# A Hymba block on one core: DVE evacuations behind each attention step's minimum, spread norm products, one key product with turned operands, and the last 256 tokens computed token-major

## The chip, the cores and the metric

The kernel runs on one core of a Trainium2 chip. TensorE (PE) multiplies, with its own weight-load queue (PEld); VectorE (DVE), ScalarE (ACT) and GpSimd (POOL) work element by element; SyncE (SP) issues nearly all DMA transfers. The metric is the device time of one execution in microseconds, the median of several runs. Lower is better.

## What is computed

One layer of a hybrid trunk on x of shape (1, 2048, 1024) in float32. Cut to what matters here:

```python
h = rmsnorm(x, norm_mix_g)
proj = h @ w_in                        # 1024 -> 512 (u) + 3 * 512 (q, k, v)
y_ssm = s5_mixer(u_ssm, ...)           # 32 groups, complex diagonal states, scan over time
y_att = chunked_attention(q, k, v, attn_rel_bias)   # 8 heads of 64; own 64-frame chunk and 8 before
x = x + concat(rmsnorm(y_ssm), rmsnorm(y_att)) @ w_out
h = rmsnorm(x, norm_ffn_g)
x = x + (silu(h @ w_gate) * (h @ w_up)) @ w_down    # inner width 2816
out = rmsnorm(x, norm_final_g)         # x * rsqrt(mean(x * x) + 1e-6) * g
```

## The kernel before

**Number format and layout.** Activations are held feature-major: features on the 128 partitions, tokens along the row. A float32 operand is split into a high part and a low part (`hi`, `lo`, in a rounded type), and a product is three matmuls, hi·hi, hi·lo and lo·hi (`mm3`, L76). `split` (L153) makes the two parts: ACT casts, DVE subtracts.

**Stages.** A state-space prologue runs to about 125 us, attention from there to about 700 us, the output projection to about 935 us, gate and up products to about 1780 us, and the down products to 2203 us. A tail of 37 us follows.

**Attention.** There are 128 steps: 4 blocks of 512 tokens, 4 head pairs, 2 heads, 4 query tiles. A step makes the scores of a query tile (2 to 4 matmuls into the bank `sc`, which has one buffer). One DVE instruction (L881) then adds the bias `nba` or `nbb`, writes the result `s` and leaves each row's minimum `mn`, and ACT takes the exponential (L884) with that minimum as its bias. In the same step PE transposes an earlier step's `s` (L79), ACT and DVE split the transposed tile into `pth` and `ptl` (L899, L900), and PE multiplies these with v. The bank `sc` is free for the next scores once L881 has read it.

**Fillers.** Between the parts of a step PE works on "units", generators that are advanced to a quota at each step by tables of step numbers:

- `hT_unit` prepares the next block's normalised input for eight feature tiles q = 0 to 7. It loads x, multiplies it by the gain and by 1/rms (L756, called the norm product here), casts to `hi` on ACT (L757) and subtracts to `lo` on DVE (L758). q = 0 to 2 have two sets of buffers, q = 3 to 7 have one. So `hi` 3 to 7 of the next block can be written only after the current block's last product that reads them.
- `qk_unit` makes the queries and the keys of a head pair (24 matmuls each, in a bank `pf` of two), then evacuates them. In the first block a DVE product with 1/rms comes first (`yt`, L791). Then ACT copies the high part and DVE subtracts the low part (L800 and L801 for q, L806 and L807 for k). A query's halves are copied to the other 64 partitions by DMA.
- `v_unit` does the same for v (L838 to L842). In the first block weights arrive raw (`raw`, two buffers, L702), are split (L153) and are written back for later blocks (`wss`). The v weights of the second half of the heads are pieces 9 and 11.
- The state-space units run their scans on POOL and a few products on PE.

**What sets the order.** PE's order is the order of the program text (`keep_in_program_order`). DVE, ACT, POOL and SP are ordered by a scheduler, by readiness and priority. An engine runs its instructions strictly in that order, so one that waits holds up all behind it.

**The tail.** The down products of the second half's last four slices run by token ranges: `TAIL = (0, 512), (512, 256), (768, 256)`. In each range `down` makes eight feature tiles and DVE adds each to `acc` (L1582). ACT squares it (L1596, L1599) and DVE sums the squares (L1600). `sums` multiplies them by ones on PE, and `newton` (L98 to L111) takes the inverse root on DVE with 14 small instructions: a first guess by integer arithmetic and three rounds. PE spreads it over the partitions (`no`), ACT copies it, and eight DVE products (L1612) and eight DMAs (L1613) finish the range:

```python
def products(self):
    pb = next(self.r)
    rs = self.rs or pb
    for i, a in enumerate(self.acc):
        v = a[:, self.ts]
        nc.vector.scalar_tensor_tensor(v, v, k.go[:, i : i + 1], rs[:, : self.n], op0=ALU.mult, op1=ALU.mult)
        nc.sync.dma_start(io["out"][i * P : (i + 1) * P, self.out], a[:, self.ts])
```

For the last range these two steps come after the last down product, with nothing else left for PE.

## Time and profile before

| | us |
|---|---|
| three runs | 2241.45, 2242.87, 2247.27 |
| median | 2242.87 |
| profiled execution | 2241.38 |
| its span | 2239.6 |
| what lies around the span | 1.8 |
| mean granted PE clock | 0.988 |

PE is busy nearly everywhere: of 40 equal slices of the span only a few show less than nine tenths, and these lie before 700 us and at the end. Its mean granted clock is read as a share of full speed; a stretch of idle time is sometimes followed by a stretch at a lower clock. Idle time of DVE, ACT and POOL costs nothing by itself. Read for each place which engine's wait ends last.

### The profile page before, as it was taken

The numbers are of one execution on the slowest core, as the hardware profiler recorded it, in microseconds if no ns is written. First come the engines' busy times: TensorE is split into PE (matmuls) and PEld (weight loads), VectorE is DVE, ScalarE is ACT, GpSimd is POOL, SyncE is SP. The second block draws the span as 40 slices with busy tenths as digits, with TensorE's granted clock in tenths as the row PEclk, the third lists the DMA queues.
The fourth block names the chain that finished last, engine by engine and source line by source line (L and its number), as shares of the span: only waits on it lengthen the run. The fifth ranks groups of instructions, "written<-read, shape, count | busy, mean of one in ns | idle before, by whom it ended". The sixth has DMA issues, their size and how long they took to land.

```text
span 2239.6 us, 30165 instructions
## 1 busy us (share of the span) xinstructions
PE 2153.6 (96%) x10632; PEld 1819.1 (81%) x10632; DVE 1543.1 (69%) x2706; ACT 1004.6 (45%) x1667; POOL 354.1 (16%) x830
## 2 busy tenths in 40 slices
PE   8988898999988999999999999999999999999997
PEld 6777797999977788788888887888888788888886
DVE  8756767555557666767766768767665577688776
ACT  6355565556567541443333335333333343353322
POOL 3354666666600000000000000000000100000000
PEclk9999999999999999999999999999999999999999
DMA  9778867666552436835645557546333495465642
GB/s 330 231 249 283 270 207 229 193 196 193 179 175 99 137 116 206 275 118 173 198 153 200 198 191 258 199 160 207 108 115 97 136 371 198 159 226 183 217 174 76
DMA packets 194664, 430.16 MB, mean 192 GB/s; under 512 B 19792, under 2 KB 38272, under 8 KB 187408
## 3 DMA queue, kind: packets, MB, share of 16 engines
q1 hardware_dynamic: 186768, 403.26, 54.3%
q0 software_dynamic: 7744, 24.97, 3.6%
q8 instruction: 83, 1.36, 0.3%
q14 instruction: 69, 0.57, 0.1%
HBM read 288.95 MB, written 131.10 MB: 188 GB/s over the span
## 4 chain that ended last, share of the span: by engine, by line
PE 81%; DMA 7%; DVE 6%; ACT 2%; issue 2%; SPq 1%; DVEq 0%; ACTq 0%
PE X L76 20%; PE ps L76 18%; PE pf L76 11%; PE Y L76 10%; PE big L76 7%; PE W L76 5%; PE pj L76 4%; PE pt L79 2%; PE sc L76 2%; DMA acc<-x 1%; DMA hd<-wc 1%; DMA x<-xt 1%; DMA lo<-hc 1%; DMA w<-wss 1%; DVE ptl L900 0%
## 5 line engine op out<-in xcount | busy, mean ns | idle before, releaser
L76 PE MATMUL X<-hi,c 128*128 128x512 f32 x1408 | 450.9, 391 | 6.5 <-DVE c L153 3.4
L76 PE MATMUL ps<-hd,hd 128*128 128x512 f32 (+1 forms) x1968 | 428.1, 379 | 3.3 <-DVE hd L153 2.0
L76 PEld LDWEIGHTS ps<-hd,hd 128*128 128x128 f32 x1968 | 356.4, 188 | 73.6 <-DVE hd L153 2.7
L76 PEld LDWEIGHTS X<-hi,c 128*128 128x128 f32 x1408 | 264.9, 188 | 63.6 <-DVE c L153 4.5
L76 PE MATMUL X<-lo,c 128*128 128x512 f32 x704 | 274.7, 390 | 0.0
L153 ACT CAST hd<-hd 128x1536 fp32r<-128x1536 f32 (+1 forms) x106 | 147.5, 1394 | 231.0 <-DMA hd<-hq 174.6
L76 PE MATMUL Y<-hi,c 128*128 128x512 f32 x704 | 225.2, 390 | 2.4 <-DVE u L1428 2.4
L153 DVE TENSOR_TENSOR hd<-hd 128x1536 fp32r<-128x1536 f32 (+1 forms) x106 | 174.1, 1644 | 38.6 <-ACT hd L153 38.3
L1532 POOL DMA_DIRECT2D hd<-hq x7 | 5.3, 757 | 1165.3 <-PE X L76 1151.2
L153 DVE TENSOR_TENSOR c<-S,c 128x512 fp32r<-128x512 f32 x176 | 120.9, 688 | 99.3 <-ACT c L153 99.0
L1424 ACT COPY u<-X 128x512 f32<-128x512 f32 x132 | 77.5, 588 | 197.4 <-PE X L76 197.3
L153 ACT CAST c<-S 128x512 fp32r<-128x512 f32 x176 | 109.4, 622 | 120.8 <-PE Y L76 61.8
L76 PE MATMUL big<-m,woh 128*128 128x512 f32 x512 | 161.5, 397 | 0.0
L76 PEld LDWEIGHTS Y<-hi,c 128*128 128x128 f32 x704 | 132.6, 188 | 31.0 <-DVE u L1428 3.2
L1566 DVE TENSOR_TENSOR acc<-acc,ps 128x512 f32<-128x512 f32 x196 | 130.1, 682 | 37.9 <-PE ps L76 37.7
L76 PEld LDWEIGHTS X<-lo,c 128*128 128x128 f32 x704 | 132.7, 188 | 27.4
L153 ACT CAST c<-raw 128x512 fp32r<-128x512 f32 x132 | 82.2, 623 | 150.2 <-PE Y L76 73.0
L76 PE MATMUL pf<-hi,w 128*128 128x512 f32 x416 | 148.7, 409 | 0.0
L76 PE MATMUL Y<-lo,c 128*128 128x512 f32 x352 | 137.2, 390 | 0.0
L900 DVE TENSOR_TENSOR ptl<-pt,pth 128x640 fp32r<-128x640 f32 (+3 forms) x152 | 98.3, 647 | 54.6 <-ACT pth L899 53.1
L884 ACT ACTIVATE s<-s,mn 128x640 f32<-128x640 f32 (+4 forms) x128 | 97.9, 765 | 61.9 <-DVE mn L881 58.6
L899 ACT CAST pth<-pt 128x640 fp32r<-128x640 f32 (+3 forms) x152 | 83.7, 551 | 83.2 <-PE pt L79 78.8
(451 smaller groups left out, 4269.1 us busy)
## 6 DMA issues: line engine op xcount, KB each, us to landing
w<-wss SPq DMA_DIRECT2D x36, 1024.0 KB, 6.2
hq<-g SPq DMA_DIRECT2D x140, 256.0 KB, 2.1
hd<-hq SPq DMA_DIRECT2D x35, 768.0 KB, 4.4
hd<-wc SPq DMA_DIRECT2D x35, 768.0 KB, 5.8
raw<-in_w_gate SPq DMA_DIRECT2D x44, 512.0 KB, 3.7
raw<-in_w_up SPq DMA_DIRECT2D x44, 512.0 KB, 4.1
wc<-px SPq DMA_DIRECT2D x66, 256.0 KB, 3.1
wss<-w SPq DMA_DIRECT2D x12, 1024.0 KB, 6.1
```

Source lines behind the costliest of these rows:

```text
L76: return self.tc.keep_in_program_order(self.tc.nc.tensor.matmul(*a, **b))
L79: return self.tc.keep_in_program_order(self.tc.nc.tensor.transpose(*a, **b))
L153: return nc.scalar.copy(hi, raw), nc.vector.tensor_tensor(lo, raw, f32(hi), op=ALU.subtract)
L884: nc.scalar.activation(s[:, :nk], s[:, :nk], AF.Exp, bias=mn[:], scale=-1.0, accum_out=sums[sb, pr][:, hh, qp : qp + 1])
L899: nc.scalar.copy(pth[:, a:b, qp, :], pt[:, a:b, :])
L900: nc.vector.tensor_tensor(ptl[:, a:b, qp, :], pt[:, a:b, :], f32(pth[:, a:b, qp, :]), op=ALU.subtract)
L1424: nc.scalar.copy(u[:], ps[:])
L1532: (nc.gpsimd if aside else nc.sync).dma_start(f32(lo), src.rearrange("g p c -> p g c"))
L1566: V.tensor_tensor(a, a, ps[:], op=ALU.add)
```

## The change

Five things change.

1. **`behind`.** Each step's L881 instruction is remembered in `k.least`. DVE instructions traced inside `behind()` are placed, in issue order only, after the most recent one: the splits of the v weights 9 and 11, the evacuations of q, k and v, and for the third and fourth block the norm products and the subtractions to `lo`.
2. **First block.** The raw v weights 9 and 11 are loaded two steps earlier, and their splits come a step apart.
3. **Third and fourth block.** The norm products of q = 3 to 7 are taken out of the loop with the casts: they run alone, spread over steps −20 to −10 before the block, and casts and subtractions follow in one step, −9. q = 0 to 2 move to steps −26 to −20.
4. **Last key product of a block** (`pr == 3`, `c == 1`): operands are read in the order q = 3 to 7, then 0 to 2.
5. **Tail.** The last 256 tokens are computed token-major by `by_tokens`, 128 tokens at a time: two banks of 512 features, into which PE also adds `acc` by a float32 product with the identity. The sum of squares comes from ACT's accumulation, the root from ACT's square root refined by four DVE instructions, and the rows go out through an output of their own (`out_t`). The other two ranges of the second half use `root` (ACT's square root and five DVE instructions) in place of `newton`. The final gain is loaded as a row on all partitions (`g_row`) before the tail, and a one-column square root ahead of it brings ACT's table.

```diff
+def root(k, pool, ps, n, w):
+
+    V = k.nc.vector
+    v, f, y, o = (k.t(pool, t, [P, w], bufs=2) for t in ("nv", "nf", "ny", "no"))
+    k.nc.scalar.activation(o[:], ps, AF.Sqrt, scale=1.0 / n, bias=k.eps)
+    V.tensor_scalar(v[:], ps, -0.5 / n, -0.5 * EPS, op0=ALU.mult, op1=ALU.add)
+    return refine(V, v, f, y, o)
+
+
+def refine(V, v, f, y, o):
+
+    V.reciprocal(y[:], o[:])
+    V.tensor_tensor(f[:], y[:], y[:], op=ALU.mult)
+    V.tensor_tensor(f[:], f[:], v[:], op=ALU.mult)
+    V.scalar_tensor_tensor(o[:], f[:], 1.5, y[:], op0=ALU.add, op1=ALU.mult)
+    return o
...
+        def behind(on=True):
+            return tc.issue_after(k.least) if on and k.least else nullcontext()
...
-                    with tc.high_priority(offset=-WAY):
+                    if n == 11:
+                        yield
+                    with tc.high_priority(offset=-WAY), behind(ns == (9, 11)):
...
+            def scaled(q):
+                with behind(sb > 1):
+                    nc.vector.scalar_tensor_tensor(xts[q], xts[q], k.gm[:, q : q + 1], S["rsn"][:, ts], op0=ALU.mult, op1=ALU.mult)
+
+            ahead = q0 and sb > 1
+            if ahead:
+                for q in range(q0, q1):
+                    yield
+                    scaled(q)
...
+                if not ahead:
+                    scaled(q)
+                nc.scalar.copy(hi[q], xts[q])
+                with behind(ahead):
+                    nc.vector.tensor_tensor(lo[q], xts[q], f32(hi[q]), op=ALU.subtract)
...
-                    for q in range(KT):
+                    qs = [*range(DB, KT), *range(DB)] if c and pr == 3 else range(KT)
+                    for n, q in enumerate(qs):
...
-                    nc.vector.tensor_tensor(t[:], ps[:], S["rsn"][:, :SB], op=ALU.mult)
+                    with behind():
+                        nc.vector.tensor_tensor(t[:], ps[:], S["rsn"][:, :SB], op=ALU.mult)
...
+                a, b = HTA if sb == 1 else HTE
+                units.append(Unit(hT_unit(sb, 0, DB), 2 + DB, g0 + a, g0 + b, 2))
+                gen, n = hT_unit(sb, DB), KT - DB
+                if sb > 1:
+                    units.append(Unit(islice(gen, 1 + n), 1 + n, g0 + HTE[1], g0 + HTM, 2))
...
+                    pre, mid = (6, (3, 2)) if c == 4 else (4, (2,))
...
+        def by_tokens(t0, hs, ds, acc):
+
+            ts = slice(t0, t0 + P)
+            m = (t0 // P) % 2
+            ps = [bank(dx) for _ in range(2)]
...
+            for c in range(2):
+                for n, ((hh, hl), (dh, dl)) in enumerate(zip(hs, ds)):
+                    mm3(te, ps[c][:], hh[:, 0, ts], hl[:, 0, ts], dh[:, 0, c * 512 : c * 512 + 512], dl[:, 0, c * 512 : c * 512 + 512], n == 0, n == len(hs) - 1, skip_group_check=True)
+                    if n == 0:
+                        for i in range(4):
+                            te.matmul(ps[c][:, i * P : (i + 1) * P], acc[4 * c + i][:, ts], k.ident[:], start=False, stop=False, skip_group_check=True)
+                    if n % 2:
+                        yield
...
+                    nc.scalar.activation(j[:], ps[c][:], AF.Square, accum_out=sq[c][:])
...
+                nc.scalar.activation(o[:], sq[1][:], AF.Sqrt, scale=1.0 / D, bias=f[:])
+                V.tensor_scalar(v[:], sq[1][:], -0.5 / D, y[:], op0=ALU.mult, op1=ALU.add)
+                refine(V, v, f, y, o)
+                nc.scalar.activation(ta, ta, AF.Copy, scale=o[:])
+                V.scalar_tensor_tensor(b[:], ps[1][:], o[:], g[:, 512:], op0=ALU.mult, op1=ALU.mult)
...
-        last.sums(True)
-        last.products()
+        for n, _ in enumerate(chain.from_iterable(by_tokens(t0, hs, ds, acc) for t0 in TOKENS)):
+            if n == 2:
+                last.sums(root=root)
+            if n == 5:
+                last.products()
```

The change moves instructions on DVE. The first place is the first block around step 12, where the scores of a new head pair meet the end of a key product. `yt` and `k` are the key's evacuation, `w` the subtractions of the v weights' split, and `s`, `mn` the step's minimum. DVE before:

```order
L900 TENSOR_TENSOR ptl_2115<-pt_2210,pth_2114 128x2x128
L791 TENSOR_TENSOR yt_2224<-pf_2069,rsn_91 128x512
L807 TENSOR_TENSOR k_406_1959<-yt_2224,k_406_1959 64x512
L807 TENSOR_TENSOR k_409_1962<-yt_2224,k_409_1962 64x512
L153 TENSOR_TENSOR w_2175<-raw_2073,w_2175 128x512 x2
L153 TENSOR_TENSOR w_2180<-raw_2075,w_2180 128x512 x2
L881 ISA s_2206,mn_2207<-sc_2203,nbb_1549 128x128
L881 ISA mn_2207 128x1
L881 ISA s_2247,mn_2248<-sc_2244,nbb_1549 128x256
```

And DVE after, at the same place:

```order
L942 TENSOR_TENSOR ptl_2116<-pt_2211,pth_2115 128x128
L175 TENSOR_TENSOR w_2128<-raw_1975,w_2128 128x512
L942 TENSOR_TENSOR ptl_2116<-pt_2211,pth_2115 128x2x128
L175 TENSOR_TENSOR w_2128<-raw_1975,w_2128 128x512
L175 TENSOR_TENSOR w_2133<-raw_1977,w_2133 128x512 x2
L922 ISA s_2207,mn_2208<-sc_2204,nbb_1550 128x128
L922 ISA mn_2208 128x1
L830 TENSOR_TENSOR yt_2225<-pf_2074,rsn_92 128x512
L922 ISA s_2248,mn_2249<-sc_2245,nbb_1550 128x256
L922 ISA mn_2249 128x1
L847 TENSOR_TENSOR k_406_1960<-yt_2225,k_406_1960 64x512
```

The key's three evacuations, which stood ahead of the minimum, now stand behind it; the four subtractions of `w` still stand ahead of it.

The second place is the end of the second block, where the third block's `lo` tiles and the last pair's keys are made. Here the scores of the next step need both `k` tiles. DVE before:

```order
L758 TENSOR_TENSOR lo_995_4534<-raw_4438,hi_994_4533 128x512
L900 TENSOR_TENSOR ptl_4418<-pt_4469,pth_4417 128x5x128
L910 RECIPROCAL rs_4625<-sm_4011 128x8
L756 SCALAR_TENSOR_TENSOR xt_5999<-xt_5999,g_mix_87,rsn_91 128x512
L758 TENSOR_TENSOR lo_997_4539<-raw_4438,hi_996_4538 128x512
L758 TENSOR_TENSOR lo_1015_4596<-raw_4440,hi_1014_4595 128x512
L807 TENSOR_TENSOR k_920_4236<-pf_4357,k_920_4236 64x512
L758 TENSOR_TENSOR lo_1017_4601<-raw_4440,hi_1016_4600 128x512
L881 ISA s_4515,mn_4516<-sc_4510,nba_97 128x640
L881 ISA mn_4516 128x1
L807 TENSOR_TENSOR k_923_4239<-pf_4357,k_923_4239 64x512
```

And after:

```order
L942 TENSOR_TENSOR ptl_4430<-pt_4475,pth_4429 128x5x128
L795 TENSOR_TENSOR lo_984_4503<-raw_3792,hi_983_4502 128x512
L795 TENSOR_TENSOR lo_986_4507<-raw_3792,hi_985_4506 128x512
L847 TENSOR_TENSOR k_930_4264<-pf_4374,k_930_4264 64x512
L795 TENSOR_TENSOR lo_988_4511<-raw_3794,hi_987_4510 128x512
L795 TENSOR_TENSOR lo_990_4515<-raw_3794,hi_989_4514 128x512
L847 TENSOR_TENSOR k_933_4267<-pf_4374,k_933_4267 64x512
L922 ISA s_4541,mn_4542<-sc_4536,nba_98 128x640
L922 ISA mn_4542 128x1
```

The norm product `xt` is gone from this place (it stands many steps earlier) and one `lo` fewer stands between `ptl` and the first `k`, but two `lo` and the second `k` now stand ahead of the next minimum.

The third place is the end of PE's queue. `ps` is the bank, `hd` the operands, `sa` and `sb` the sums of squares, `no` the inverse root. PE before:

```order
L76 MATMUL ps_19989<-hd_19522,hd_19526 128x256 x3
L76 MATMUL ps_19990<-hd_19522,hd_19526 128x256 x3
L76 MATMUL ps_20023<-ones_85,sa_19898 128x1
L76 MATMUL ps_20023<-ones_85,sb_19901 128x1
L79 MATMUL ps_20046<-ident_80,no_20031 128x128 x2
```

And after:

```order
L79 MATMUL ps_19916<-hd_19504,hd_19500 128x512 x3
L79 MATMUL ps_19916<-ident_80,acc_3276_18347 128x128
L79 MATMUL ps_19916<-ident_80,acc_3277_18348 128x128
L79 MATMUL ps_19916<-ident_80,acc_3278_18349 128x128
L79 MATMUL ps_19916<-ident_80,acc_3279_18350 128x128
L79 MATMUL ps_19916<-hd_19512,hd_19508 128x512 x3
L79 MATMUL ps_19916<-hd_19520,hd_19516 128x512 x3
L79 MATMUL ps_19916<-hd_19528,hd_19524 128x512 x3
```

PE's queue now ends with a down product: the products with ones and the transposes of `no` for the last range are gone, and four products of `acc` with the identity stand in each bank.

More of the change, by code (lines that the diff above doesn't have):

```diff
@@ L43 @@
 HTP = 2
+HTE, HTM, HTL = (-26, -20), -10, (-9, -8)
 PRO = 0, 0, 2, 2, 2, 2, 0, 0, 0
@@ new lines, in qk_unit @@
+                with behind():
+                    for hh in range(2):
+                        q2h, q2l, k2 = ts[hh]
+                        a = slice(hh * 64, hh * 64 + 64)
+                        o = slice(64 - hh * 64, 128 - hh * 64)
+                        if c == 0:
+                            ways = (a, o) if both and hh == 0 else (a,)
+                            for w in ways:
+                                nc.scalar.activation(q2h[w, :], ps[a, :], AF.Copy, scale=-0.125)
+                                nc.vector.scalar_tensor_tensor(q2l[w, :], ps[a, :], -0.125, f32(q2h[a, :]), op0=ALU.mult, op1=ALU.subtract)
+                            if len(ways) == 1:
+                                nc.sync.dma_start(f32(q2h[o, :]), f32(q2h[a, :]))
+                                nc.sync.dma_start(f32(q2l[o, :]), f32(q2l[a, :]))
+                        else:
+                            nc.scalar.copy(k2[a, -SB:], ps[a, :])
+                            nc.vector.tensor_tensor(k2[o, -SB:], ps[a, :], f32(k2[a, -SB:]), op=ALU.subtract)
+                            if sb < NSB - 1:
+                                nc.sync.dma_start(S["k"][sb % 2, 2 * pr + hh], f32(k2[:, -SB:]))
```

120 lines of the change are left out of this document (64 added, 56 removed).

## The prediction

> **What bounds the kernel now.** I read the page's busy shares first, then its chain of waits by engine.
>
> ```profile
> span 2239.6 us, 30165 instructions
> PE 2153.6 (96%) x10632; PEld 1819.1 (81%) x10632; DVE 1543.1 (69%) x2706; ACT 1004.6 (45%) x1667; POOL 354.1 (16%) x830
> PE 81%; DMA 7%; DVE 6%; ACT 2%; issue 2%; SPq 1%; DVEq 0%; ACTq 0%
> ```
>
> PE is busy for 96% of the span and has 81% of the chain. So the change can win in two ways: it fills places where PE waits, or it shortens what follows PE's last matmul. Attention's places are found with a table of windows (columns: stretch, its length, busy time and count of PE, PEld, DVE, ACT, POOL, then PE's clock, DMA share, GB/s) and with PE's rows in the timeline; a bracket there gives the idle time before the row and who ended it.
>
> ```profile
> 177.70:183.40 5.70, 0.00 (x0) 0.01 (x1) 4.83 (x10) 3.50 (x7) 5.21 (x16) 0.88 1.01 372
> 183.40:189.00 5.60, 5.57 (x26) 5.60 (x27) 1.28 (x4) 1.64 (x6) 4.97 (x12) 0.51 1.01 383
> 275.70:282.00 6.30, 6.30 (x35) 5.58 (x36) 5.08 (x9) 3.74 (x9) 1.30 (x3) 1.00 0.56 171
> 370.00:374.00 4.00, 4.00 (x15) 3.50 (x16) 3.47 (x6) 2.00 (x4) 3.88 (x6) 0.60 0.61 212
> 400.00:650.00 250.00, 249.69 (x1592) 229.01 (x1591) 135.75 (x245) 137.79 (x274) 138.81 (x351) 1.00 0.60 182
> ...
> 183.43 0.55 PE L76 MATMUL sc<-k,q2h 128*128 128x256 f32 x1 [5.74 <-DVE mn L881]
> 275.67 0.77 PE L79 MATMUL pt<-ident,s 128*128 128x128 f32 x5 [3.11 <-DVE ptl L900]
> 369.93 0.63 PE L76 MATMUL sc<-k,q2h 128*128 128x320 f32 x1 [4.08 <-DVE k L807]
> 385.92 0.76 PE L79 MATMUL pt<-ident,s 128*128 128x128 f32 x5 [1.41 <-DVE ptl L900]
> ```
>
> From 400 to 650 us PE stands still for 0.3 us, so nothing is to be won there. Before that there are four stalls, all ended by DVE: 5.74 us (A), 3.11 (B), 4.08 (C) and 1.41 (D). After A the clock granted is 0.51, after C 0.60, and after B's 3.11 us it stays 1.00. So a stall costs more than its length from somewhere between 3.1 and 4.1 us on.
>
> [...]
>
> **Stall A, first block.** Behind what did the minimum wait?
>
> ```profile
> 177.72 0.69 DVE L791 TENSOR_TENSOR yt<-pf,rsn 128x512 f32<-128x512 f32 x1
> 179.10 1.40 DVE L807 TENSOR_TENSOR k<-yt,k 64x512 fp32r<-64x512 f32 x2 [0.68 <-ACT k L806]
> 180.53 2.54 DVE L153 TENSOR_TENSOR w<-raw,w 128x512 fp32r<-128x512 f32 x4
> 182.99 0.28 DVE L881 CUSTOM_DVE_ANT_0 s<-sc,nbb 128x128 f32<-128x128 f32 x1
> ...
> 163.67 0.64 SPq L729 DMA_DIRECT2D wss<-w  x1
> 174.21 1.07 SPq L702 DMA_DIRECT2D raw<-in_w_v  x2
> ...
> raw<-in_w_v SPq DMA_DIRECT2D x4, 512.0 KB, 6.4
> ...
> 175.32 4.51 DMA nbb<-nbs
> 185.05 3.84 PE pf L76 x18
> 190.63 2.15 PE pf L76 x18
> ```
>
> DVE spent 177.72 to 183.07 on the key's evacuation (0.69 + 0.68 idle + 1.40) and on four subtractions of the split (2.54); only then came the minimum. By the order of the changed kernel the evacuation stands behind the minimum. The four subtractions still stand ahead of it, but their data come earlier: the raw loads stand in SP's queue right behind the write of `wss` at 163.67, so they go out near 164.3 and not at 174.21, and at the median 6.4 us from issue to landing they are there at about 171. The subtractions then fall into the steps around 173 to 177. What is left is the bias `nbb`, which lands at 175.32 + 4.51 = 179.8, perhaps 1 us sooner without the raw issues ahead of it. The minimum then ends at 179.2 to 180.0 and not 183.2: 3.2 to 4.0 us. The rest of the stall, 1.7 to 2.5 us, is below B's length, which kept the clock, so 18 matmuls cost 2.15 and not 3.84: 1.7 more. Sum 4.9 to 5.7; I take **5.0**, since the DMA share is 1.01 there and transfers can be late. Bounds: 0 if the raws land as late as before, 7.4 (5.74 + 1.7) if all of it goes.
>
> **Stalls B, C, D, third and fourth block.**
>
> ```profile
> L756 DVE SCALAR_TENSOR_TENSOR raw<-raw,g_mix,rsn x12: 739/746/2143, 230.0 to 383.6; 128x512 f32<-128x512 f32 x12
> 271.14 2.14 DVE L756 SCALAR_TENSOR_TENSOR raw<-raw,g_mix,rsn 128x512 f32<-128x512 f32 x1
> 274.03 0.85 DVE L756 SCALAR_TENSOR_TENSOR raw<-raw,g_mix,rsn 128x512 f32<-128x512 f32 x1
> 365.17 1.08 DVE L756 SCALAR_TENSOR_TENSOR xt<-xt,g_mix,rsn 128x512 f32<-128x512 f32 x1
> 366.17 2.99 DVE L758 TENSOR_TENSOR lo<-raw,hi 128x512 fp32r<-128x512 f32 x2
> 369.19 0.68 DVE L807 TENSOR_TENSOR k<-pf,k 64x512 fp32r<-64x512 f32 x1
> ```
>
> B: two norm products of the third block (271.14 and 274.03) run directly ahead of the `ptl` at 274.80 for which PE waits. In the changed order they stand some 20 steps before their block, each behind a minimum, and none is left here. Of 3.11 us I take **2.8**; bounds 0 and 3.11.
>
> C: ahead of the first `k` stand a norm product (1.08) and two `lo` (2.99). Now the product is gone and two `lo` remain, which start where the product did: `k` ends near 368.0 and not 369.87, so the stall falls from 4.08 to about 2.2, and below B's length the clock stays: 0.40 of the 4.0 us window at 0.60, 1.6 us. Against it stands a new cost: `lo` twice and the second `k` now stand ahead of the next minimum, where one `lo` stood; two instructions of 0.7 us, of which I charge 1.0. Sum 1.9 + 1.6 − 1.0 = **2.5**; bounds 0 and 5.7 (4.08 + 1.6). That `lo` 3 to 7 can start sooner, because the turned key product lets go of `hi` 3 to 7 earlier, is in this.
>
> D: the products at the fourth block's `x` tiles go the same way: 1.41 and a smaller wait of 0.3 beside it, 1.7; I take **1.5**; bounds 0 and 1.7.
>
> New: the moved products and subtractions take DVE time elsewhere. It has 135.75 us of work in the 250 us from 400 on, so they find room, and I charge 0.8; bounds 0 and 3. What hides the evacuations' delay of one minimum is PE's own work: a unit's product runs 24 matmuls while the other `pf` bank is read. Attention in all: 5.0 + 2.8 + 2.5 + 1.5 − 0.8 = **11.0**.
>
> Unchanged, since the order around them is: a wait for `Bst` of 2.6 us and three of 14.1 us in all for `ptl` in the output projection.
>
> ```profile
> PE pj L76 <- DMA Bst<-bsts: 2.6, 1, 2.6
> PE pt L79 <- DVE ptl L900: 14.1, 3, 6.6
> ```
>
> **The tail.**
>
> ```profile
> 961.06 5.44 PE X L76 x24
> 279.03 1.24 PE L76 MATMUL pj<-rsn,Bst 128*128 128x256 f32 x5
> 2207.59 0.65 PE L79 MATMUL ps<-ident,no 128*128 128x128 f32 x4 [1.21 <-DVE no L110]
> 2222.03 0.43 PE L79 MATMUL ps<-ident,no 128*128 128x128 f32 x2 [1.40 <-DVE no L110]
> 2222.21 3.12 PE L76 MATMUL ps<-hd,hd 128*128 128x256 f32 x24
> 2208.24 9.44 PE ps L76 x80
> 2229.75 0.16 DVE L108 TENSOR_TENSOR nf<-ny 128x2 f32<-128x2 f32 x1
> 2232.32 3.22 DVE L1612 SCALAR_TENSOR_TENSOR acc<-acc,g_final,ps 128x256 f32<-128x256 f32 x8 [0.85 <-PE ps L79]
> 2187.34 0.64 ACT L1599 ACTIVATE sg<-acc 128x512 f32<-128x512 f32 x1 [0.65 <-DVE sa L1600]
> L884 ACT ACTIVATION_READ_ACCUMULATOR s<-s,mn x128: 183/188/196, 129.5 to 694.9; 128x1 f32 x128
> ```
>
> PE's time: the last range's 96 matmuls of 256 columns at 0.1235 (between 9.44 / 80 = 0.118 in the chain and 3.12 / 24 = 0.130 in the timeline) are gone, 11.9 us. In their place come 48 of 512 columns at 5.44 / 24 = 0.227, 10.9 us, and 16 float32 products of 128 columns. A float32 matmul shows as two passes in this trace (the `pj` row: 1.24 us for 5 passes of 256 columns, about 0.215 from start to start), so 32 passes. For one of 128 columns I take half, 0.115, 3.7 us; bounds 3.2 (0.10) and 6.9 (0.215, if the width does not matter). Net −11.9 + 10.9 + 3.7 = +2.7 us. The wait of 1.40 for the middle range's root falls, since `root` has 5 small DVE instructions where `newton` has 14 and PE now has a bank of work ahead of it: net cost **1.3**. The wait of 1.21 for the first range's root falls in the same way: **1.2** won.
>
> After the last matmul: before, it ends at 2222.21 + 3.12 = 2225.33 and the last DVE product at 2232.32 + 3.22 = 2235.54, 10.2 us. Now follow a square of 512 columns with its accumulator (0.64 + 0.19), a one-column root (about 0.2, by the accumulator's read), four small DVE instructions at 0.2 from start to start, and one product of 512 columns (0.75 by the norm product), with about 0.1 for handing over: 2.7. Won **7.5**; the closing DMAs are two of 256 KB in place of eight of 128 KB, with a landing as long. Tail: 1.2 − 1.3 + 7.5 = **7.4**; bounds 2.5 (float32 passes at 0.215 and a chain of 4.4 us) and 8.5. The load of `g_row` ahead of the first gate operands and one load of ACT's table in front of the tail I cost at nothing, hidden behind PE's products; without cover they cost 1.6 and 1.3.
>
> **The sum.** 11.0 + 7.4 = 18.4 us less than the profiled execution's 2241.38 (span 2239.6 and 1.8 around it): 2223.0. That execution lies 1.5 below the median of 2242.87, so against the runs it is about 2224.5; I say **2225**.
>
> **The rivals.** (1) *Only the tail gains.* Stalls A to C come back under another name: the four subtractions of `w` still stand ahead of the minimum in the order, and the raws must land in a stretch where the DMA share is 1.01; in C `lo` still stands ahead of `k`. Attention then gives 0 to 3, the time is 2242.9 − 7.4 − 1.5 = 2234 (2231 to 2237). Against it: the raws go out 10 us earlier. Chance 0.17.
>
> (2) *The tail gives 3 only*, with the float32 passes at 0.215 and a longer end: 2242.9 − 11 − 3 = 2229. Chance 0.10; it lies within the range.
>
> (3) *Spread norm products run long.* The group above has a median of 746 ns and a maximum of 2143: one took 1.4 us longer, and POOL is at work through most of attention (138.81 of 250 us in the table). There are 16 such products now, spread to places where PE has no slack. If each costs half of that, 16 × 0.7 = 11, attention gives nothing: 2235. Against it: a product behind a minimum has most of a step to finish. Chance 0.08.
>
> [...]
>
> (4) *Slower: evacuations pile up at the bank `pf`.* Each of the 32 q and k products is now evacuated behind a minimum (0.9 us with its read). If PE always stood at the next bank for that long, 32 × 0.9 = 29 would be lost against 18 won: about 2254. It decides from 18.4 / 32 = 0.58 us a product on. Against it: the order shows few evacuations that changed sides, and there are two banks with 24 matmuls (5.4 us) between. Chance 0.05.
>
> **How the numbers follow.** Forecast 0.60, rivals 0.17, 0.10, 0.08 and 0.05. 0.3% of the median is 6.7 us, about what a measurement of this kernel can tell from no change; faster means below 2236.1. The forecast and rival 2 lie below it, of rivals 1 and 3 about two thirds: 0.60 + 0.10 + 0.16 = 0.86, of which I take off 0.03 for a cost that no row shows. Faster 0.83, same 0.10, slower 0.07. The forecast's own range is 2216 to 2231, from bounds of A, C and the tail; to hold the time 8 times in 10 it reaches up to rivals 1 and 3: **2215 to 2237**.
>
> **What would show it.** In the changed profile: the wait of 5.74 for the minimum shrinks below 3 us and the clock behind it stays at 1.00 (A); no norm product next to a `ptl` that PE waits for at 272 and 385 (B, D); a wait for `k` near 370 of about 2 us without a slower clock (C); about 2.7 us from the last matmul to the last DVE product (tail), and the last 16 float32 products at 0.115 a pass. It would be wrong if a new wait on `sc`, `pf` or `pt` of several microseconds appears in the second to fourth block, or if the raws still land after 177.

## The result, and the profile after

| | before | changed |
|---|---|---|
| six runs, median (us) | 2243.26 | 2233.45 |
| six runs, lowest and highest | 2241.45 and 2247.41 | 2226.24 and 2236.52 |
| profiled execution | 2241.38 | 2226.24 |
| span | 2239.6 | 2224.1 |

The ratio of the changed kernel to the one before is 0.9938, with an interval of 0.9924 to 0.9951: faster by 0.6%, or some 14 us. The two medians in the table lie closer together, 9.8 us, so the size is less sure than the direction. The profiled execution is the fastest of its six, 7 us below their median, and its span is 15.5 us shorter than the span before. The kernel before scatters too, from 2240.84 to 2249.61 us in the 36 runs beside the experiments, and its profile is one of its fast executions as well. The distance between the changed kernel's profile and its median is the main thing that the experiments had to explain.

The page of the changed kernel, span, busy shares and chain by engine:

```profile
span 2224.1 us, 30080 instructions
PE 2155.5 (97%) x10606; PEld 1817.2 (82%) x10606; DVE 1533.2 (69%) x2671; ACT 1008.0 (45%) x1675; POOL 355.7 (16%) x830
PE 82%; DVE 7%; DMA 5%; issue 2%; ACT 2%; SPq 1%; ACTq 0%; DVEq 0%
```

PE is busy 1.9 us longer than before in a span that is 15.5 us shorter, so about 17 us of its idle time are gone. Where the four stalls were, PE's rows of the timeline now read:

```profile
180.20 0.36 PE L79 MATMUL sc<-k,q2h 128*128 128x256 f32 x1 [2.70 <-DVE mn L922]
226.40 1.96 PE L79 MATMUL pj<-U,Bst 128*128 128x256 f32 x8 [0.41 <-DMA Bst<-bsts]
234.14 0.50 PE L79 MATMUL pj<-pth,v 128*128 128x512 f32 x1 [2.14 <-ACT pth L941]
361.20 0.41 PE L79 MATMUL sc<-k,q2h 128*128 128x320 f32 x1 [2.31 <-DVE k L847]
```

A is 2.70 us and not 5.74, C is 2.31 and not 4.08; B and D have no row of a microsecond or more. A wait for `pth` of 2.14 us at 234 is new. The tail, in the timeline's rows of PE, ACT and DVE:

```profile
2214.47 1.05 PE L79 MATMUL ps<-ident,acc 128*128 128x128 f32 x8
2215.28 2.32 PE L79 MATMUL ps<-hd,hd 128*128 128x512 f32 x9
2217.63 0.60 ACT L1683 ACTIVATE sg<-ps 128x512 f32<-128x512 f32 x1 [2.97 <-PE ps L79]
2219.52 0.75 DVE L1694 SCALAR_TENSOR_TENSOR ob<-ps,no,rsn 128x512 f32<-128x512 f32 x1
```

Eight passes of the float32 product start at 2214.47 and the next product at 2215.28, so a pass costs 0.10 us. The last matmul ends at 2215.28 + 2.32 = 2217.60 and the last DVE product at 2220.27: 2.7 us in place of 10.2.

**Where the time went, stretch by stretch.** To compare profiles, time is taken between the same events: the ends of the 128 minima (numbered from 0), the first copy of a gate product by ACT, and the 207th addition to `acc` on DVE. Three profiles of the changed kernel are shown, its own and two more that were taken later (the first and the tenth experiment).

| stretch (us) | before | changed | again | third | won | forecast |
|---|---|---|---|---|---|---|
| minimum 11 to 14 (A) | 17.0 | 11.9 | 14.3 | 13.1 | 5.0, 2.7, 3.9 | 5.0 |
| 19 to 27 | 36.3 | 38.0 | 39.2 | 38.1 | −1.7, −2.9, −1.8 | 0 |
| 33 to 38 (B) | 28.3 | 25.1 | 29.0 | 25.5 | 3.2, −0.7, 2.8 | 2.8 |
| 55 to 58 (C) | 16.5 | 13.2 | 13.1 | 13.7 | 3.3, 3.4, 2.8 | 2.5 |
| 58 to 89 (D) | 141.2 | 140.2 | 140.2 | 140.1 | 1.0, 1.0, 1.1 | 1.5 |
| 121 to the first gate copy | 284.6 | 288.0 | 288.2 | 287.4 | −3.4, −3.6, −2.8 | 0 |
| 207th addition to the end (tail) | 37.3 | 29.7 | 29.7 | 29.7 | 7.6, 7.6, 7.6 | 7.4 |
| whole span | 2239.6 | 2224.1 | 2230.1 | 2229.6 | 15.5, 9.5, 10.0 | 18.4 |

The tail gives the same in every profile. A and B vary, and two stretches that the forecast took as unchanged lose 2 to 4 us each in these three profiles.

### The profile page after: what moved, and what is told of

It is laid out like the page before. It is cut to its first block, busy times and chain, and to the rows that moved or that the text cites. A ratio compares the mean times of both kernels' runs of the same rounds, so it can differ in the third digit from the quotient of the medians.

```text
span 2224.1 us, 30080 instructions
## 1 busy us (share of the span) xinstructions
PE 2155.5 (97%) x10606; PEld 1817.2 (82%) x10606; DVE 1533.2 (69%) x2671; ACT 1008.0 (45%) x1675; POOL 355.7 (16%) x830
## 4 chain that ended last, share of the span: by engine, by line
PE 82%; DVE 7%; DMA 5%; issue 2%; ACT 2%; SPq 1%; ACTq 0%; DVEq 0%
PE X L79 21%; PE ps L79 19%; PE pf L79 11%; PE Y L79 10%; PE big L79 6%; PE W L79 5%; PE pj L79 4%; PE sc L79 2%; PE pt L82 2%; DMA acc<-x 1%; DMA hs<-g 1%; DVE lo L175 1%; DMA lo<-hc 1%; DMA x<-xt 0%; DVE ptl L942 0%
## 5 line engine op out<-in xcount | busy, mean ns | idle before, releaser
L175 DVE TENSOR_TENSOR hd<-hd 128x1536 fp32r<-128x1536 f32 (+1 forms) x106 | 174.2, 1646 | 38.5 <-ACT hd L175 38.1
L1616 DVE TENSOR_TENSOR acc<-acc,ps 128x512 f32<-128x512 f32 x196 | 130.6, 684 | 39.2 <-PE ps L79 38.7
L941 ACT CAST pth<-pt 128x640 fp32r<-128x640 f32 (+3 forms) x152 | 83.7, 551 | 76.9 <-PE pt L82 72.2
```

The costliest lines, as they stand in the source:

```text
L175: return nc.scalar.copy(hi, raw), nc.vector.tensor_tensor(lo, raw, f32(hi), op=ALU.subtract)
L941: nc.scalar.copy(pth[:, a:b, qp, :], pt[:, a:b, :])
L1616: V.tensor_tensor(a, a, ps[:], op=ALU.add)
```

## The experiments

Each run has runs of the kernel before on the same chip beside it. Ratios are to those. The intervals of most experiments overlap with those of the changed kernel (0.9924 to 0.9951, 0.9915 to 0.9946, 0.9922 to 0.9956); there the traces carry the argument, one profile for each, and not the times.

**1. The changed kernel again.** No edit.

> The changed kernel once more, nothing edited. In its first six runs the time went from 2226.2 to 2236.5 while the mean granted clock went from 0.989 down to 0.984, and the one profile that there is belongs to the fastest. Theory (clock windows): one slow window of 3.41 us costs 1.7 us, so runs 7 us apart differ by about four such windows, and a profile of a slower run shows them as stretches of clock 0.50 that the first profile does not have, behind stalls of 2 to 4 us. Then times scatter again over some 10 us, with the clock falling by 0.001 for each 2.2 us. Rival (transfers): the runs differ by transfers that land late; then a slower profile has longer waits for DMA at the same clock, and time and clock are not tied.

Measured: 2224.19 to 2235.43 us, median 2230.41, against 2246.59 before; ratio 0.9930 (0.9915 to 0.9946). The profile has a span of 2230.1 us at a mean clock of 0.987. Its stall A is as long as in the first profile:

```profile
179.97 0.55 PE L79 MATMUL sc<-k,q2h 128*128 128x256 f32 x1 [2.78 <-DVE mn L922]
```

2.78 us against 2.70, yet 2.3 us more are lost there. The table of windows shows why (columns: stretch, its length, busy time and count of PE, PEld, DVE, ACT, POOL, PE's clock, DMA share, GB/s). The windows are cut where the granted clock changes, on a grid of 3.413 us: in the profiles before and after every stretch at one clock lasts 3.413 us or a multiple of it, from 3.413 to 846.5, but for the last one. First the first profile of the changed kernel:

```profile
175.17:178.58 3.41, 1.92 (x9) 1.34 (x9) 2.78 (x7) 2.45 (x6) 3.02 (x11) 1.00 0.87 296
178.58:181.99 3.41, 1.79 (x15) 1.82 (x16) 3.15 (x9) 1.91 (x6) 3.02 (x11) 1.00 0.60 223
181.99:185.41 3.42, 3.42 (x25) 3.02 (x24) 2.05 (x6) 1.89 (x6) 3.03 (x12) 1.00 0.58 213
```

And the same place in this run:

```profile
175.81:179.22 3.41, 1.38 (x6) 0.77 (x5) 2.86 (x6) 2.61 (x6) 3.02 (x10) 1.00 0.98 368
179.22:182.64 3.42, 2.67 (x12) 2.70 (x13) 3.01 (x8) 2.48 (x7) 3.03 (x10) 0.50 0.30 111
182.64:186.05 3.41, 3.41 (x17) 3.41 (x16) 0.86 (x3) 0.48 (x1) 2.94 (x13) 0.50 0.88 324
186.05:189.46 3.41, 3.41 (x28) 3.32 (x27) 1.84 (x5) 1.94 (x5) 3.17 (x4) 1.00 1.00 396
```

In the first profile the grid cuts the stall in two: PE is busy for 1.92 and 1.79 us of the windows, 56% and 52%, and the clock stays. Here the stall falls into one window with 1.38 us busy, 40%, and the two windows behind it run at 0.50. Counted over the twelve profiles, all 77 full-clock windows in which PE is busy for up to 0.41 are followed by a slow one, 19 of the 43 between 0.41 and 0.50 are, and above that 22 of some 7500 (the last section comes back to these). The grid does not start with the program: its place differs from profile to profile (a window begins at 175.17 us of the span there, at 175.81 here). So whether stalls of one length (2.70 and 2.78 us here, 3.11 and 3.13 under experiment 2) cost only that or some 1.5 to 3.0 us more (an estimate: half of PE's busy time in the slow windows behind them, 2.98 us there, 2.67 + 3.41 here) is decided by where the grid happens to lie.

The other losses of this profile, in its table of waits (in total, times, longest):

```profile
PE pj L79 <- DMA Bst<-bsts: 2.1, 1, 2.1
PE pj L79 <- ACT X L613: 2.4, 1, 2.4
```

Bst came 1.7 us later after PE than in the first profile, and behind B's place a wait for `X` of the state-space units appeared. (ACT's copy to `X` waits 7.12 us for the transfer `XG`, which POOL issues; in the first profile it waits 4.68.) So the rival (transfers) has a part, but the smaller one (see the last experiment). Time and clock are tied as expected: of the 18 runs of the changed kernel in this study those at a mean clock of 0.989 took 2224.2 to 2228.6 us, those at 0.984 to 0.986 took 2231.7 to 2236.5.

**2. The tail alone.** The kernel before with part 5 of the change only.

> The kernel before with the change's tail alone (token-major end, the new root, the gain's row and the early table load), attention as before. Theory: the terms add, so the tail gives 7.4 us of its own: about 2236 against 2243 before, with 2.7 us from the last down product to the last DVE product. The load of the gain's row costs about 1.5 us of this ahead of the first gate product, if that is what lengthened the wait there from 1.8 to 3.4 us: then 2237. Rival: the tail's gain depends on work that the attention part moves, or is eaten by clock: under 3 us.

Measured: 2237.13 against 2246.59, ratio 0.9970 (0.9954 to 0.9986), about 6.7 us. The stretch of the tail is 29.7 us, as in the changed kernel. Stall B, which is untouched here, shows the clock once more. Its row, and the windows behind it:

```profile
275.59 1.33 PE L81 MATMUL pt<-ident,s 128*128 128x128 f32 x5 [3.13 <-DVE ptl L920]
```

```profile
271.74:275.15 3.41, 0.73 (x6) 0.48 (x5) 3.35 (x4) 1.09 (x3) 3.32 (x4) 1.00 0.86 277
275.15:278.57 3.42, 2.98 (x10) 2.60 (x11) 3.42 (x7) 1.51 (x3) 1.78 (x3) 0.50 0.49 118
```

3.13 us, nearly the same stall that in the profile before (3.11 us) left the clock at 1.00, is punished here: 0.73 of 3.41 us busy. In the profile before the grid had cut it in two, with PE busy for 1.80 and 1.92 us (53% and 56%):

```profile
270.76:274.18 3.42, 1.80 (x11) 1.22 (x9) 3.36 (x5) 1.61 (x3) 3.38 (x5) 1.00 0.93 322
274.18:277.59 3.41, 1.92 (x11) 1.70 (x12) 3.41 (x6) 1.12 (x2) 2.74 (x4) 1.00 0.52 162
```

**3. The attention part alone.** The kernel before with parts 1 to 4 only.

> The kernel before with the change's attention part alone (issue order behind the minimum, earlier raw loads, spread norm products, turned last key product), tail as before. Theory: 11 us are won by the end of attention, as in the changed kernel's profile, and nothing is lost ahead of the first gate product since the gain's row is not loaded: 2232 to 2234. If the clock windows of the slower runs come with the attention part, the runs scatter over some 10 us here, and not in the run with the tail alone. Rival: most of the 11 us come back in the output projection, 2238 or more.

Measured: 2238.47 (2234.13 to 2242.11), ratio 0.9967 (0.9953 to 0.9981), about 7.4 us and not 11. The time is the rival's (2238 or more), but not for its reason: from minimum 121 to the first gate copy this profile takes 283.7 us, 0.9 less than before, so nothing comes back in the output projection. The two ratios add up: 0.0030 + 0.0033 = 0.0063, and the whole change has 0.0061 to 0.0070 in its three comparisons. Stall A is as in the changed kernel,

```profile
181.58 0.54 PE L77 MATMUL sc<-k,q2h 128*128 128x256 f32 x1 [2.71 <-DVE mn L902]
```

but its row takes 0.54 us and not 0.36: a slow window stands behind it. In this profile A to D win 4.0, 2.7, 3.3 and 1.0 us, 11.0 in all as expected. PE is idle for 9.1 us less than before (86.0 and 76.9), while 2.7 us more go to the slow clock. The runs scatter over 8 us, with the tail alone over 7, and the 13 runs of the kernel before beside them over 8; so the scatter does not come with the attention part.

**4. No issue order.** One line:

```diff
-            return tc.issue_after(k.least) if on and k.least else nullcontext()
+            return nullcontext()
```

> The changed kernel without the issue order: evacuations, late splits and products go where the scheduler puts them, all else as changed (early raw loads, spread products, turned product, tail). Theory: of stall A the key's evacuation (0.7 us and 1.4 us, with its wait for ACT 2.8 us) comes back ahead of the minimum, so the stall is about 5 us again, with the slow clock behind it: 4 us slower than the changed kernel, and up to 6 with other places. Rival: the earlier raw loads alone removed the stall, and the order is worth less than 1 us.

Measured: 2235.12, ratio 0.9952 (0.9938 to 0.9966). The stalls A and C in the timeline:

```profile
182.38 0.55 PE L79 MATMUL sc<-k,q2h 128*128 128x256 f32 x1 [4.93 <-DVE mn L922]
...
373.45 0.63 PE L79 MATMUL sc<-k,q2h 128*128 128x320 f32 x1 [4.62 <-DVE k L847]
```

4.93 us for A, as expected (2.2 more than with the order), and C is 4.62 against 2.31. The order is worth about 2.2 us at each place, plus the slow windows, which stand behind both stalls here; the early loads alone did not remove A. In the runs it is 0.0013 to 0.0022 of the ratio, some 3 to 5 us, as expected in size, with overlapping intervals.

**5. Raw weights late.** The order stays, the loads go back:

```diff
-                    if n == 11:
-                        yield
-                    pre, mid = (6, (3, 2)) if c == 4 else (4, (2,))
+                    pre, mid = 4, (2,)
```

> The changed kernel with the raw v weights 9 and 11 loaded and split at the steps of the kernel before; the issue order stays. Theory: the key's evacuation stays behind the minimum, but the raws land after 176 and the four subtractions wait for them ahead of the minimum: stall A is 4.5 us or more, against 2.7 with the early load, and always has a slow window behind it: 2 to 4 us slower than the changed kernel by the end of the first block. Rival: the minimum is held by the bias nbb alone, then the stall stays at 2.7 us.

Measured: 2232.65 (2230.1 to 2238.7), ratio 0.9948 (0.9931 to 0.9965). PE's stall, and DVE ahead of it:

```profile
181.68 0.49 PE L79 MATMUL sc<-k,q2h 128*128 128x256 f32 x1 [4.40 <-DVE mn L920]
...
178.50 1.32 DVE L175 TENSOR_TENSOR w<-raw,w 128x512 fp32r<-128x512 f32 x2 [1.13 <-ACT w L175]
180.03 1.29 DVE L175 TENSOR_TENSOR w<-raw,w 128x512 fp32r<-128x512 f32 x2 [0.20 <-ACT w L175]
```

4.40 us, with a slow window behind it, as expected: the minimum stands behind four subtractions that wait for the split's high parts. So A is short only with both, the order (4.93 without) and the early loads (4.40 without); what the last 2.7 us are is said below. In the runs the difference is 2 to 4 us, less than the intervals tell apart.

**6. Products not spread.** The norm products back at their old steps, still behind a minimum:

```diff
-            ahead = q0 and sb > 1
+            ahead = False
-                a, b = HTA if sb == 1 else HTE
+                a, b = HTA
-                if sb > 1:
+                if False:
-                a, b = HTS if sb == 1 else HTL
+                a, b = HTS
...
```

> The changed kernel with the third and fourth block's norm products at the steps of the kernel before, together with their casts and subtractions; the issue order behind the minimum stays for the products. Theory: the waits for the transposes at 272 (3.1 us before, 0 in the changed kernel) and 385 (1.4 us) come back in part, and the stall at k near 368 grows from 2.3 to 4 us: 3 to 6 us slower than the changed kernel. Rival: the issue order alone keeps these places free and the spread is worth under 1 us.

Measured: 2236.33 (2232.22 to 2240.58), ratio 0.9957 (0.9943 to 0.9972), some 4 us slower than the changed kernel. That is the expected size, but by luck, since the place is another one. PE's wait and DVE's row ahead of it:

```profile
374.86 0.79 PE L79 MATMUL pf<-lo,w 128*128 128x512 f32 x1 [3.58 <-DVE lo L795]
...
370.00 3.35 DVE L778 SCALAR_TENSOR_TENSOR raw<-raw,g_mix,rsn 128x512 f32<-128x512 f32 x2
```

With the products behind a minimum and not ahead of it, `k` at C is not late any more (its wait is 1.3 us); other norm products run late instead, two of them in 3.35 us, and the next block's first product waits 3.58 us for `lo`. The expected waits for the transposes at 272 and 385 did not come back. So in this profile the order alone moves the stall on, and the spread removes it.

**7. The gain's row late.**

```diff
-        nc.sync.dma_start(S["rsn"][:, :D], ...)
+        with tc.issue_after(k.sent.ins):
+            nc.sync.dma_start(S["rsn"][:, :D], ...)
```

Here `k.sent` is the last output transfer of the first half.

> The changed kernel with the load of the gain's row queued behind the first half's output transfers, far behind the first gate product. Theory: the row's 512 KB ahead of the loads that the first gate product needs delay it; without them the wait there is 1.4 to 1.8 us, as in the kernel before and with the attention part alone, and not 2.9 to 3.4: 1.5 us faster. Rival: that wait comes from elsewhere and stays near 3 us.

Measured: 2229.62 (2228.61 to 2232.28), ratio 0.9932 (0.9919 to 0.9945). The changed kernel itself has 0.9930, 0.9938 and 0.9939, so no difference shows. The wait ahead of the first gate product:

```profile
PE X L79 <- DVE xt L1198: 2.9, 1, 2.9
```

It is 2.9 us without the row ahead of it; with the row it was 3.4, 3.0 and 1.9 in the three profiles, and 1.6 in the fourth experiment. The theory falls: the row is not needed for a wait near 3 us. What lengthens it was not found.

**8. PE kept busy.** Products of the identity with itself, whose result nothing reads, ahead of waiting instructions.

```diff
+    def busy(self, n, out):
+        for _ in range(n):
+            self.te.matmul(out, self.ident[:], self.ident[:], start=True, stop=True, skip_group_check=True)
...
+            k.busy(BUSY_K.get(steps.index(st), 0), ps[:, 1, :P])
```

> The changed kernel with products of the identity with itself (128 columns, 0.2 us each, into banks whose content is overwritten afterwards) placed ahead of PE instructions that wait: 12 at the first scores, 8 at stall A, 7 at the scores of the last head pair in the first two blocks, 24 and 20 at the two long waits for transposes near 650 us, 8 at the first root of the output projection, 12 each at the first gate product of the two halves. Nothing else changes. Theory (clock windows): on a grid of 3.41 us, a window in which PE works less than about half of the time is followed by one or more at half clock; with PE busy in the stalls the slow windows at 127, 180, 222, 650 to 690, 721, 929 and 1370 us go away. Each costs about 1.7 us where PE is the bound, so the time falls by 6 to 12 us against the changed kernel, and the runs scatter over less than 6 us and not over 10. Rival: the slow clock follows the length of a stall of useful work or has another cause; then the added products change nothing or cost up to 3 us where the stall is shorter than they are.

Measured: 2233.44 (2229.16 to 2240.04), ratio 0.9954 (0.9940 to 0.9969): no faster than the changed kernel, with a mean clock of 0.994. The slow windows at 127, 180, 222, 721, 929 and 1370 are gone, as the theory has it, though some between 646 and 684 us stay. But the added products cost as much: against the first profile of the changed kernel (split into kinds of time as under the tenth experiment) the clock loss is 6.8 us smaller and the idle time 14.3, and PE's other busy time 24.3 larger. The runs still scatter over 10.9 us, not under 6 as expected. Two causes of the cost show. At the long waits near 650 us, the windows of the two stalls of the changed kernel,

```profile
650.70:657.20 6.50, 0.03 (x1) 0.00 (x0) 3.36 (x7) 6.45 (x8) 0.00 (x0) 0.68 0.51 172
659.50:665.40 5.90, 0.15 (x2) 0.07 (x2) 5.28 (x10) 5.87 (x11) 0.00 (x0) 0.50 0.37 142
```

and of this run,

```profile
654.20:660.80 6.60, 5.58 (x50) 5.38 (x48) 3.56 (x7) 6.55 (x8) 0.00 (x0) 1.00 0.51 175
662.00:669.00 7.00, 4.67 (x43) 4.51 (x42) 6.36 (x11) 6.96 (x13) 0.00 (x0) 1.00 0.51 166
```

show ACT busy for nearly all of them (the fourth number): ACT is the bound there, and a PE at full clock is not through any sooner. And where the products stood at a place without a stall (the first gate product of the second half), their 2.8 us were lost.

**9. Fewer of them**, at other places: none near 650 us, at the root that PE does wait for, and at the up product of the second half.

```diff
+            if steps.index(st) == 13:
+                k.held = k.t(pfs, "pf", [P, 256])
+                k.busy(8, k.held[:, :P])
...
                 ps = big()
+                k.busy(8, ps[:, :P])
                 spread(k, te, ps[:, :512], b.o[1], 0)
...
+                if busy:
+                    k.busy(busy, bank("W")[:, :P])
```

> As the run that kept PE busy, with the added identity products only where PE itself is the bound, and fewer: 12 at the first scores, 8 at stall A (into the bank that the next product takes anyway), 7 each at the scores of the last head pair in the first two blocks, 8 at the spread root of the output projection's first block, 7 at the first gate product, 9 at the first up product of the second half; none at the two long waits near 650 us, which DVE and ACT bound, and none where the run before lost their whole length. Theory: the clock loss (work done in half-clock windows, halved) falls from 17 to 22 us to about 10 as there, idle time and added products together do not grow by more than 2 us, so 5 to 8 us faster than the changed kernel on the same chip. Rival: the added products again cost what the clock gives back, within 2 us.

Measured: 2226.15 (2219.90 to 2233.24) against 2244.58 before, ratio 0.9915 (0.9898 to 0.9932); the changed kernel beside it on the same chip has 2232.53 and 0.9939. That is 6.4 us by the medians, and this is the fastest version of the study. The intervals overlap, so the gain over the changed kernel is likely and not certain, and the runs scatter over 13.3 us. Its clock and span, and the first scores in the timeline of PE:

```profile
core 0: 2223.3 us, clock 0.992
```

```profile
123.08 2.84 PE L80 MATMUL sc<-ident 128*128 128x128 f32 x24
127.35 0.33 PE L80 MATMUL sc<-hi2x,hi0x 128*128 128x128 f32 x1 [1.43 <-DVE hi2x L852]
```

PE still waits until 127.35 for `hi2x`, which comes no earlier, but the score product takes 0.33 us and not 0.42, and the 11 steps behind it take 42.1 us and not 43.9. Some of the gain is given back: in the first block ACT now waits for a weight,

```profile
195.17 1.14 ACT L180 CAST w<-raw 128x512 fp32r<-128x512 f32 x2 [1.71 <-DMA raw<-in_w_qk]
```

and a stall of 2.6 us for `ptl` follows. With PE ahead, the raw weights' transfers become the bound there in this profile.

**10. The changed kernel a third time**, beside the ninth.

> The changed kernel a third time, beside the run above on the same chip. Theory: its profile again splits into the same useful work (2139 us of PE), idle time of 68 to 72 us, and a clock loss that differs by up to 5 us from profile to profile; what the clock loss differs by is most of what the spans differ by. Rival: the spans differ by idle time, at the same clock loss.

Measured: 2232.53 (2224.89 to 2236.22), ratio 0.9939 (0.9922 to 0.9956). For this comparison the trace of each profile is split in three: PE's idle time (the span less its busy time), the clock loss (PE's busy time in half-clock stretches, halved: in the changed kernel's slow window at 929.5 us the gate products of 512 columns start 0.43 us apart, at full clock behind it 0.23), and the rest, which is useful work at full clock.

| us | before | changed | again | third | kept busy, fewer |
|---|---|---|---|---|---|
| span | 2239.6 | 2224.1 | 2230.1 | 2229.6 | 2223.3 |
| idle | 86.0 | 68.6 | 70.9 | 67.5 | 61.1 |
| clock loss | 17.7 | 16.8 | 21.6 | 26.2 | 12.0 |
| the rest | 2135.9 | 2138.7 | 2137.6 | 2135.9 | 2150.2 |

The changed kernel's first profile and its third differ by 5.5 us in span: the clock loss is 9.4 us larger, idle time 1.1 and the rest 2.8 smaller. Between the first and the second the clock loss makes 4.8 of 6.0 us. So the clock loss is what differs most, but not as the expectation has it: it differs by 9.4 us and not by up to 5, "the same useful work" varies by 3 us, and between the second and the third the spans are 0.5 us apart with 4.6 between their clock losses. In the ninth run the rest holds the added products, 11 to 14 us of them, 6 to 10 us of it in place of idle time.

## Why the prediction was right, and which step was wrong

The time lies inside the range, faster as forecast, but some 8 us above the middle of it, and as near to the first rival's 2234 as a number can be. So the number does not decide between them; the stretches do. A to D together win 12.5, 6.4 and 10.6 us in the three profiles, where that rival left attention 0 to 3 us and the forecast has 11.8.

Sorted by the kinds of time in the table above, the forecast amounts to 17.8 us less idle time, 3.3 less clock loss (1.7 for A, 1.6 for C) and 2.7 more work in the tail. The three profiles have 17.4, 15.1 and 18.5 us less idle time; the clock loss is 0.9 smaller, 3.9 larger and 8.5 larger; the rest is 2.8, 1.7 and 0.0 larger. So the idle time came nearly as forecast, and the miss is the clock. By the prediction's own steps:

- **The tail** was right in each term: 7.6 us for 7.4. The passes of 128 columns cost 0.10 (taken 0.115, bounds 0.10 and 0.215), the end chain 2.7 for 2.7, and PE's work there is 2.7 us longer as worked out. Rival 2 falls.
- **A** was right in what it needs: experiments 4 and 5 show that it needs both parts, as the prediction had it, and the raw weights landed at 170.4 and 171.6, for "about 171". But the wait that ends last was misread. The prediction left the bias `nbb` last, at 179.8; in the trace its two transfers, issued at 174.01 and 174.65, land by 178.0. Last is the split: its casts on ACT begin only at 176.29, 4.7 us after the weights had landed, and stand behind a cast that waited for PE:

```profile
176.13 0.27 ACT L941 CAST pth<-pt 128x128 fp32r<-128x128 f32 x1 [1.45 <-PE pt L82]
176.29 0.62 ACT L175 CAST w<-raw 128x512 fp32r<-128x512 f32 x1
177.08 1.67 ACT L175 CAST w<-raw 128x512 fp32r<-128x512 f32 x3
177.89 1.95 DVE L175 TENSOR_TENSOR w<-raw,w 128x512 fp32r<-128x512 f32 x3
179.77 0.28 DVE L922 CUSTOM_DVE_ANT_0 s<-sc,nbb 128x128 f32<-128x128 f32 x1
```

That the minimum still ended at about 180.0, where the forecast had it, is luck in this respect, and so is the 5.0 us of the stretch: its idle time fell by 3.0 us (3.3 taken) and its clock loss by 2.7 (1.7 taken), while 0.7 us more of other work lies in it. The stall left is 2.7 us, where 1.7 to 2.5 were worked out.
- **B, C, D**: 3.2, 3.3 and 1.0 us in the first profile for 2.8, 2.5 and 1.5; together 7.5 for 6.8. The waits for `k`, 2.31 us where about 2.2 was expected, were read well from DVE's queue. In the second profile B gives nothing: with the stall at `ptl` gone, a wait of 2.4 us for `X` takes its place, where ACT's copy waits 7.12 us for POOL's transfer and not 4.68.
- **The step that failed** is in what bounds the kernel: "So a stall costs more than its length from somewhere between 3.1 and 4.1 us on." It was drawn from one row, B's 3.11 us with a clock of 1.00 behind it. Experiment 1 shows 2.78 us punished and experiment 2 B's 3.13; a row of the profile before spoke against it too, 1.84 us ahead of the first gate product with a slow window behind it:

```profile
936.23 0.64 PE L76 MATMUL X<-hi,c 128*128 128x512 f32 x1 [1.84 <-DVE xt L1148]
...
936.36:939.78 3.42, 3.38 (x8) 2.18 (x9) 2.73 (x5) 1.68 (x3) 0.00 (x0) 0.50 0.96 255
```

What decides, by the windows counted under experiment 1 and by the stalls filled in experiments 8 and 9, is for how much of a 3.413 us window PE works: up to 41% is followed by a slow window in 77 of 77 cases, more than half in 22 of some 7500. The 2.78 us of experiment 1 were punished though they are shorter than a window, with PE busy for 40% of it. From the step that failed came the 1.7 us for A and the 1.6 for C, as if a shorter stall were always free. They are won in some executions only, and the stalls that remain (2.1 to 3.0 us, four to six of them ahead of 400 us in each profile) are punished in others. In the three profiles the clock loss is 2.4, 7.2 and 11.8 us above what the forecast left of it (17.7 less 3.3).
- **"Unchanged, since the order around them is"** was the second miss. From minimum 19 to 27 the changed kernel needs 1.7 to 2.9 us more in all three profiles. The wait for `Bst` is not a new cost: it was 2.6 us before, and is 0.4, 2.1 and 3.0. New are a wait for `pth` of 2.1 us in the first two profiles and, in the third, a slow stretch of two windows where the kernel before has one. With the raw weights late (experiment 5) the stretch takes 36.3 us, as before; the cause stays open. From 121 to the first gate copy 2.8 to 3.6 us are lost. Most of this is the clock, whose loss there grows by 2.3 to 3.7 us; idle time grows by 1.2 at most. In the profiles of experiments 3, 4, 7 and 9 the stretch takes 283.7 to 284.6 us, no longer than before, so the change does not always cost this. The cause of the longer wait ahead of the first gate product stays open.
- **Rivals.** The fourth (evacuations pile up at `pf`) did not show: no wait for a bank of `pf` of a microsecond is in the profile. Of the third, the first half shows: the 16 spread norm products take 0.75 to 1.81 us. But PE does not wait for them: it is idle for 0.4 us between minimum 38 and 55 and for 1.2 between 58 and 89, where they stand (0.0 and 2.5 before). The first is half right: the stalls A and B come back in some executions, though shorter.

## What to carry to other kernels

Read a stall of PE together with the granted clock of the next two windows, and in more than one profile: stalls of 2.70 and 3.11 us were free here in one execution, and stalls of 2.78 and 3.13 at the same places cost some 1.5 to 3.0 us more in another, so a single profile gives neither the threshold nor the median. When a stall is removed, ask what PE then reaches too early; some of the gain can come back there as a wait for a transfer, as for `X` at B here. Where PE had to wait and was itself the bound afterwards, products that nobody reads held the clock (a mean of 0.994 and 0.992 in the profiles of experiments 8 and 9, against 0.985 to 0.989 in the changed kernel's three). At a place without a stall they cost their length, 2.8 us, and near 650 us, where ACT is busy for 6.55 of 6.60 us, PE at full clock was not through any sooner.

## What the runs showed of the hardware that was not expected

- The granted clock changes on a grid of 3.413 us. A window in which PE is busy for up to 41% is followed by a slow one (77 of 77 in the twelve profiles), and of windows between 41% and 50% some are (19 of 43); in the profiles before and after, the nine slow stretches of each ahead of 2200 us end with a window in which PE is busy for 85% to 100%.
- In the output projection windows 82% and 93% busy by the trace, with 14 or 16 products of a single column (the sums by ones) in them, are followed by a slow one in several profiles (82% at 748.6 us before, 82% at 738.4 in the changed kernel's first profile). Counted without these products, the same windows are 33% to 43% busy, and of all windows over half busy only 2 of some 7470 are followed by a slow one, not 22. That such products count little as work would fit this; it was not tried by itself.
- With float32 products of 128 columns in the stalls, windows near 127 and 180 us stay at 1.00: the first score product behind them takes 0.33 us near 127 (experiment 9; 0.42 in the changed kernel's first profile), and the one near 180 takes 0.36 (experiment 8), as in that first profile, and not 0.55 and 0.54 as with a slow window behind the stall (experiments 1 and 3).
